# The choice of keys in a sparse-attention block: ties ranked by a running sum instead of position rounds

## The chip, the cores and the metric

The kernel runs on one core of a Trainium2 chip. A core has a matrix engine (TensorE, PE in the profile), three engines for elementwise work (VectorE or DVE, ScalarE or ACT, GpSimd or POOL) and a queue for memory transfers (SyncE, SP). Each engine takes its own instructions in order; semaphores let one engine wait for another. The metric is the device time of one execution in microseconds.

## What is computed

The block takes 1024 tokens of width 1024 through a norm and one input projection; its columns go to two mixers. One is a sparse attention: for each query a small indexer scores all keys, and the 256 keys of the highest score are kept, within the limit of the query's chunk. The other is a gated linear attention (GLA) with a recurrence over chunks. The output projection and a gated feed-forward network follow. The part that the change touches is this (of the reference):

```python
dots = jax.nn.relu(jnp.einsum('bqhd,bsd->bqhs', qib, k_idx_f) * IDX_DIM ** -0.5)
score = jnp.einsum('bqhs,bqh->bqs', dots, wb * IDX_HEADS ** -0.5)
score = jnp.where(key_pos[None, None, :] < limit, score, NEG)
_, sel = lax.top_k(score, topk)          # topk = 256
valid = sel < limit
```

Of equal scores, `top_k` keeps those of the lower position. Equal scores are frequent, because a ReLU makes many scores exactly zero.

## The kernel before

**Tiles.** The 1024 queries stand in 8 tiles of 128 partitions. `acc[t]` holds the scores of tile `t`, one row per query; its width `NA[t]` is the number of admissible keys: nothing to choose for tiles 0 and 1, then 384, 512, 640, 768, 1024 and 1024 columns for tiles 2 to 7.

**The choice.** `choose(ts)` (L739) finds for three tiles together, bit by bit, the 256th highest score of each row. It runs twice: group A is tiles 2, 5, 6 (384, 768 and 1024 columns), group B tiles 3, 4, 7 (512, 640, 1024). One round, `counts` (L758), counts for the current threshold how many scores are not below it: DVE counts the first two tiles (L756, a compare whose accumulator sums the hits), ACT the third, as a sum of signs (L762). Two compares (L776, `bit`, one for DVE's tiles and one for ACT's) turn counts into bits, and L788 builds the next threshold `thr`. There are 32 such rounds per group. Since a sum of signs counts an equal score half, `up` (L790) tries the next higher float for ACT's tile (`nxt`, one count on DVE, `keep` L807, and a predicated copy L808).

**Equal scores, before.** L817 and L819 rewrite `acc` in pieces of up to 512 columns: where the score equals the threshold the column's position from the constant `iota` (in units of 1/4096) takes its place. Then ten more rounds of the same `counts` on positions find how many are to be kept: `dlt` (L829, two compares) and `pos` (L834). L839 writes the mask into `acc[t]`, which the softmax later adds (L1340).

**The order of the work.** The program is recorded by a planner inside the kernel. Each part is a generator that yields an engine and a cost in ns, or a slot or an event to wait for; the planner runs a clock per engine and takes, among the parts that could start first, the one of the lowest rank. The order that comes out is fixed: each engine runs it as written. The planner's costs are estimates, and an edit that changes them shifts unrelated instructions. `choose` has rank 14 (`R_CHOOSE`), the projections 30, the GLA parts 2.5 to 4. Slots hold memory: `hp` hands out seven half tiles (128 partitions by 2 KB) that the choice shares with the GLA's elementwise parts.

**Names around the choice.** While the choice runs, PE computes projections (`pj`, `pf`; L368 to L370 are the three matmuls of one split product), the scores' products (`dots`), the gate of the GLA (`pz` L984), its cumulated decays (`bc` L1037), and its chunks (`pa` L1122, `pk` L1105, `pv` L1144). DVE empties what PE leaves: `la` (L987) reads `pz`, `spillq` (L876) reads `pf`, and `att` (L1124) masks `pa`. The results lie in a few banks: the next `pz` waits until `la` has read the one before, and `pk` waits until `att` has read `pa`. From `lg` (L1327) on come the softmax and the rest. At the start, `more_loads` (L427) issues small constants on SP's queue, `iota` (L435) among them, ahead of the input weights `st` (L247), which ACT (L257) and POOL (L262) split into two halves `w` for PE; `qi` is the first product with them.

Of the kernel before, what the change touches and what calls it, by code (L numbers as in the profile page):

```python
# [9 lines left out]
F32 = mybir.dt.float32  # L10
# [37 lines left out]
def f32(ap):  # L48
    return ap.bitcast(F32)
# [9 lines left out]
def dve(n):  # L59
    return n / 0.96 + 68  # L60
# [261 lines left out]
def block_kernel(ctx: ExitStack, tc: tile.TileContext, a: dict, out: bass.AP, dbg=None):  # L322
# [35 lines left out]
    def row_bc(ap, n):  # L358
        return bass.AP(tensor=ap.tensor, offset=ap.offset, ap=[[0, P], [1, n]])
# [66 lines left out]

    def more_loads():  # L427

        todo = [(mats[:, 1:, :], a["c_mats"][:, 1:, :]), (iot, row_bc(a["c_iota"], S)), (wgu[96:112, :], w_gu),
                   (bgt, row_bc(a["b_gate"], 256)), (gnb, row_bc(a["gla_norm"], 512)), (tab, a["rel_bias"]),  # L430
                   (nrm[:, 1, :], a["norm_ffn"].rearrange("l (k p) -> p (l k)", p=P))]
# [27 lines left out]


    wiT = cst.tile([P, NT * 8], F32, name="wiT")
    iot = cst.tile([P, S], F16, name="iota")
    fl = Flow()
    ev = fl.event
    pg = Slots(fl, NPG - NT - 1)
# [268 lines left out]
        yield ev("score", ORDER[-1])  # L734
        pg.give()

    UNIT = 1.0 / 4096.0

    def choose(ts):  # L739

        v = nc.vector
        n = len(ts)
        nv = n - 1
        nm = str(ts[0])
        cnt, pos, dlt = (cst.tile([P, n], F32, name=x_ + nm) for x_ in ("cnt", "pos", "dlt"))
        sgn, bit, thr = (cst.tile([P, n], I32, name=x_ + nm) for x_ in ("sgn", "bit", "thr"))
        lo, hi, cy, nxt, keep = (cst.tile([P, 1], I32, name=x_ + nm) for x_ in ("lo", "hi", "cy", "nxt", "keep"))
        thf = f32(thr)  # L750
        for t in ts:
            yield ev("score", t)

        def count(i, col, op):
            w = NA[ts[i]]
            v.tensor_scalar(junk_v[:, :w], acc[ts[i]], col, 0.0, op0=op, op1=ALU.add, accum_out=cnt[:, i:i + 1])  # L756

        def counts(col, op, after):  # L758

            t = ts[nv]  # L760
            e = yield ACT, act(NA[t], True), False
            nc.scalar.activation(junk_a[:, :NA[t]], acc[t], AF.Sign, bias=col[:, nv:], scale=-1.0,  # L762
                                 accum_out=cnt[:, nv:])
# [9 lines left out]
        def few(out_, val):  # L773

            def after(o, of_signs):
                v.tensor_scalar(out_[:, o], cnt[:, o], float(S - 2 * TOPK if of_signs else TOPK), val,  # L776
                                op0=ALU.is_gt if of_signs else ALU.is_lt, op1=ALU.mult)
            return after

        yield DVE, 70  # L780
        v.memset(thr, 0)
        yield from counts(thf, ALU.is_ge, few(sgn, -1.0))
        yield DVE, 70
        v.tensor_scalar(thr, sgn, 1 << 30, None, op0=ALU.bitwise_xor)
        for b in range(30, -1, -1):
            yield from counts(thf, ALU.is_ge, few(bit, float(1 << b)))
# [18 lines left out]
        count(nv, f32(nxt), ALU.is_ge)  # L805
        yield DVE, 200
        v.tensor_scalar(keep, cnt[:, nv:], float(TOPK), None, op0=ALU.is_ge)  # L807
        v.copy_predicated(thr[:, nv:], keep, nxt)  # L808
        for i, t in enumerate(ts):
            w = NA[t]  # L810
            for c0 in range(0, w, HB):
                o = slice(c0, min(w, c0 + HB))
                m = o.stop - o.start
                yield hp
                yield DVE, 2 * dve(m)
                tmp = half([P, HB], F32, "tie")
# [4 lines left out]
                hp.give()  # L821
        yield DVE, 140
        v.memset(pos[:, :nv], (1 + 512) * UNIT)
        v.memset(pos[:, nv:], (1 + 512 - 0.5) * UNIT)
        for b in range(9, -1, -1):
            step_ = float(1 << b) * UNIT

            def after(o, of_signs):
                v.tensor_scalar(dlt[:, o], cnt[:, o], float(2 * TOPK - S if of_signs else TOPK), step_,  # L829
                                op0=ALU.is_lt, op1=ALU.mult)  # L830

            yield from counts(pos, ALU.is_lt, after)
            yield DVE, 70
            v.scalar_tensor_tensor(pos, pos, -(step_ / 2 if b else step_), dlt, op0=ALU.add, op1=ALU.add)  # L834
        yield DVE, 70
        v.tensor_scalar(pos[:, nv:], pos[:, nv:], 0.5 * UNIT, None, op0=ALU.add)
        for i, t in enumerate(ts):
            yield DVE, NA[t] / 1.92 + 130
            v.tensor_scalar(acc[t], acc[t], pos[:, i:i + 1], BIG, op0=ALU.is_gt, op1=ALU.mult)  # L839
            save(f"mask{t}", acc[t])  # L840
            ev("mask", t).set()


    d_vb = [dr.tile([P, 512], F32, name=f"d_vb{i}") for i in range(NT)]
# [1407 lines left out]
def _constants():  # L2252
# [16 lines left out]
        "c_iota": ((np.arange(S, dtype=np.float32) + 1) / np.float32(4096.0)).astype(np.float16)[None, :],  # L2269
    }  # L2270


# [14 lines left out]
```

## Time and profile before

| | us |
|---|---|
| median of 3 runs (lowest, highest) | 1335.14 (1332.27, 1335.7) |
| profiled execution | 1333.15 |
| its span in the trace | 1331.3 |
| PE busy | 1268.2 (95% of the span) |
| DVE busy | 968.9 (73%) |
| ACT busy | 621.1 (47%) |
| POOL busy | 444.1 (33%) |

The profile shows one execution. Busy time counts an engine's instructions, not its waits, so an engine can be busy 95% on average and idle half of one stage. A wait is put down to the instruction that released it. The choice of keys runs from 94 to 409 us.

### The profile page before, as it was taken

How to read it: one execution, taken by the hardware profiler on the slowest of the kernel's cores; microseconds unless marked ns; L12 is line 12 of the kernel's file. 1: busy time of each engine (PE TensorE's matmuls, PEld its weight loads, DVE VectorE, ACT ScalarE, POOL GpSimd, SP SyncE). 2: the span in 40 equal slices, each digit the busy share in tenths (PEclk: the TensorE clock that was granted, in tenths of full speed). 3: DMA queues.
4: the chain of work that ended last, by engine and by line, in shares of the span. 5: the costliest groups of instructions: out<-in, count | busy, mean ns of one | idle time of the engine just before them, and what ended most of it. 6: DMA issues, size and time to landing. Idle time of an engine off the chain costs nothing.

```text
span 1331.3 us, 18081 instructions
## 1 busy us (share of the span) xinstructions
PE 1268.2 (95%) x6074; PEld 1028.8 (77%) x6074; DVE 968.9 (73%) x1900; ACT 621.1 (47%) x1139; POOL 444.1 (33%) x410
## 2 busy tenths in 40 slices
PE   5999999969999999989987999999999999999997
PEld 5878868746787888868865888888888888888886
DVE  5379998989996788724387788889776664435885
ACT  4467678554544677632143444444444432222232
POOL 4324324533311444561244343435333220000351
PEclk8999989979998999989988999999999999999999
DMA  7654221234471233565212676777667549555664
GB/s 217 182 145 127 67 60 49 95 127 167 170 233 46 74 112 112 164 209 206 87 40 80 221 263 235 269 263 266 221 222 237 182 170 381 200 197 190 206 252 174
DMA packets 122812, 230.22 MB, mean 173 GB/s; under 512 B 14120, under 2 KB 70240, under 8 KB 122720
## 3 DMA queue, kind: packets, MB, share of 16 engines
q1 hardware_dynamic: 122720, 229.07, 51.3%
q8 instruction: 48, 0.79, 0.3%
q14 instruction: 44, 0.36, 0.1%
HBM read 146.19 MB, written 82.85 MB: 172 GB/s over the span
## 4 chain that ended last, share of the span: by engine, by line
PE 75%; DVE 16%; issue 3%; DMA 2%; ACT 2%; POOL 1%; SPq 1%; POOLq 0%; DVEq 0%; ACTq 0%
DVE junk_v L756 6%; PE av L1387 3%; PE fc L1769 3%; PE fa L1769 3%; PE fa L1770 3%; PE fc L1770 3%; PE fa L1771 3%; PE fc L1771 3%; PE fb L1771 3%; PE fb L1770 3%; PE da L2085 3%; PE da L2083 3%; PE da L2084 3%; PE fb L1769 3%; PE ptr L1363 3%
## 5 line engine op out<-in xcount | busy, mean ns | idle before, releaser
L1594 POOL TENSOR_TENSOR w<-raw,w 128x512 fp32r<-128x512 f32 x66 | 96.8, 1469 | 181.9 <-ACT w L1730 140.7
L262 POOL TENSOR_TENSOR w<-st,w 128x512 fp32r<-128x512 f32 x68 | 91.3, 1350 | 88.3 <-ACT w L257 87.2
L1730 ACT ACTIVATE w<-raw 128x512 fp32r<-128x512 f32 x132 | 81.7, 626 | 63.0 <-DMA d_wd<-wd 17.1
L756 DVE TENSOR_SCALAR_CACHE_REDUCE junk_v<-acc,thr 128x640 bf16<-128x640 f32 (+3 forms) x128 | 103.6, 809 | 1.9
L762 ACT ACTIVATE junk_a<-acc,thr 128x1024 bf16<-128x1024 f32 x64 | 73.4, 1147 | 44.0 <-DVE thr L788 31.1
L2031 DVE TENSOR_TENSOR da<-U,da 128x512 fp32r<-128x512 f32 x54 | 43.9, 812 | 53.3 <-ACT da L2029 52.9
L1350 POOL TENSOR_SCALAR pb<-pb,sume 128x384 f32<-128x384 f32 (+3 forms) x64 | 47.6, 750 | 99.7 <-DVE sume L1348 79.9
L368 PE MATMUL pj<-w,hT 128*128 128x512 f32 x192 | 78.8, 410 | 1.4 <-DVE spillq L876 1.4
L2029 ACT ACTIVATE da<-U 128x512 fp32r<-128x512 f32 x54 | 33.6, 629 | 95.9 <-PE da L2085 28.2
L1769 PE MATMUL fb<-hc,w 128*128 128x512 f32 x176 | 70.4, 400 | 8.2 <-ACT w L1730 4.2
L368 PE MATMUL pf<-hT,w 128*128 128x512 f32 x192 | 76.7, 400 | 0.0
L1771 PE MATMUL fb<-hc,w 128*128 128x512 f32 x176 | 70.3, 400 | 5.7 <-DVE w L1597 5.7
L369 PE MATMUL pj<-w,hT 128*128 128x512 f32 x192 | 75.7, 394 | 0.0
L370 PE MATMUL pj<-w,hT 128*128 128x512 f32 x192 | 75.6, 394 | 0.0
L370 PE MATMUL pf<-hT,w 128*128 128x512 f32 x192 | 75.5, 393 | 0.0
L369 PE MATMUL pf<-hT,w 128*128 128x512 f32 x192 | 75.5, 393 | 0.0
L1770 PE MATMUL fb<-hc,w 128*128 128x512 f32 x176 | 70.7, 402 | 1.9 <-DVE hc L1597 1.2
L1594 POOL TENSOR_TENSOR wd<-wd 128x512 fp32r<-128x512 f32 x33 | 50.2, 1525 | 65.6 <-ACT wd L1960 60.1
L1960 ACT ACTIVATE wd<-wd 128x512 fp32r<-128x512 f32 x77 | 48.1, 628 | 49.9 <-DMA d_wd<-wd 22.3
L1769 PE MATMUL fc<-hc,w 128*128 128x512 f32 x176 | 68.7, 390 | 0.3 <-DVE gt L1818 0.3
L1769 PE MATMUL fa<-hc,w 128*128 128x512 f32 x176 | 68.7, 390 | 0.0
L2085 PE MATMUL da<-db,da 128*128 128x512 f32 x176 | 68.6, 390 | 0.0
(303 smaller groups left out, 3733.5 us busy)
## 6 DMA issues: line engine op xcount, KB each, us to landing
d_wd<-wd SPq DMA_DIRECT2D x77, 512.0 KB, 3.5
db<-d_wd SPq DMA_DIRECT2D x77, 512.0 KB, 3.4
st<-w_in SPq DMA_DIRECT2D x52, 256.0 KB, 2.8
raw<-w_ffn_gate SPq DMA_DIRECT2D x22, 512.0 KB, 5.2
raw<-w_ffn_up SPq DMA_DIRECT2D x22, 512.0 KB, 4.5
wd<-w_ffn_down SPq DMA_DIRECT2D x44, 256.0 KB, 4.9
d_ux<-gt SPq DMA_DIRECT2D x9, 512.0 KB, 2.6
d_uy<-gt SPq DMA_DIRECT2D x9, 512.0 KB, 2.8
```

The source lines that it names most:

```text
L262: self.nc.gpsimd.tensor_tensor(w[:, 1, :], st, f32(w[:, 0, :]), op=ALU.subtract)
L368: mm(ps, lh, rh, start=first, stop=False)
L369: mm(ps, lh, rl, start=False, stop=False)
L370: mm(ps, ll, rh, start=False, stop=last)
L756: v.tensor_scalar(junk_v[:, :w], acc[ts[i]], col, 0.0, op0=op, op1=ALU.add, accum_out=cnt[:, i:i + 1])
L762: nc.scalar.activation(junk_a[:, :NA[t]], acc[t], AF.Sign, bias=col[:, nv:], scale=-1.0, accum_out=cnt[:, nv:])
L1594: nc.gpsimd.tensor_tensor(dst, src, high, op=ALU.subtract)
L1730: nc.scalar.activation(w4[:, 0], src, AF.Copy)
L1769: mm(b, w[:, 0, kk], h[:, 0, :], start=first, stop=False, skip_group_check=True)
L1770: mm(b, w[:, 0, kk], h[:, 1, :], start=False, stop=False, skip_group_check=True)
L1771: mm(b, w[:, 1, kk], h[:, 0, :], start=False, stop=k == 3, skip_group_check=True)
L2085: mm(bs[t], l[:, 1, tt], r[:, 0, :], start=False, stop=last, skip_group_check=True)
```

## The change

The rounds lose one of their two compares: DVE's count now adds up in the unit of the sum of signs, so that a single compare of three columns serves all three tiles. It stands behind DVE's counts and behind ACT's. The tie passes and the ten position rounds go, with the constant `iota` and its load. In their place each tile gets a part of its own, `mask`, spawned with ranks 14, 15 and 16: ACT writes the sign of threshold minus score to a half tile (bfloat16) and sums it; DVE writes where the sign is zero to a second half tile (float16), makes a running sum of it in place, works out from both sums how many equal scores are too many, adds one to the sign where the running sum exceeds that number, and writes the mask.

```diff
 def more_loads():
-    todo = [(mats[:, 1:, :], ...), (iot, row_bc(a["c_iota"], S)), (wgu[96:112, :], w_gu),
+    todo = [(mats[:, 1:, :], ...), (wgu[96:112, :], w_gu),
...
 def choose(ts):
...
-        def count(i, col, op):
+        def count(i, col):
             w = NA[ts[i]]
-            v.tensor_scalar(junk_v[:, :w], acc[ts[i]], col, 0.0, op0=op, op1=ALU.add, accum_out=cnt[:, i:i + 1])
+            v.tensor_scalar(junk_v[:, :w], acc[ts[i]], col, float(S - TOPK), op0=ALU.is_ge, op1=ALU.subtract,
+                            accum_out=cnt[:, i:i + 1])
...
             for i in range(nv):
                 yield DVE, dve(NA[ts[i]]) + 70, False
-                count(i, col[:, i:i + 1], op)
-            yield DVE, 190
-            after(slice(0, nv), False)
+                count(i, thf[:, i:i + 1])
             yield At(e)
-            yield DVE, 70
-            after(slice(nv, n), True)
+            yield DVE, 150
+            v.tensor_scalar(out_, cnt, float(2 * TOPK), val, op0=ALU.is_gt, op1=ALU.mult)
...
         for i, t in enumerate(ts):
-            for c0 in range(0, w, HB):
...
-                v.scalar_tensor_tensor(tmp[:, :m], acc[t][:, o], thf[:, i:i + 1], iot[:, o],
-                                       op0=ALU.is_le, op1=ALU.mult)
-                v.scalar_tensor_tensor(acc[t][:, o], acc[t][:, o], thf[:, i:i + 1], tmp[:, :m],
-                                       op0=ALU.is_lt, op1=ALU.add)
...
-        for b in range(9, -1, -1):
...
-            yield from counts(pos, ALU.is_lt, after)
-            v.scalar_tensor_tensor(pos, pos, -(step_ / 2 if b else step_), dlt, op0=ALU.add, op1=ALU.add)
...
-            v.tensor_scalar(acc[t], acc[t], pos[:, i:i + 1], BIG, op0=ALU.is_gt, op1=ALU.mult)
+            fl.spawn(mask(t, thf[:, i:i + 1], cnt[:, i:i + 1], need[:, i:i + 1], eqs[:, i:i + 1]), R_CHOOSE + i)
...
+    def mask(t, thr, sg, need, eqs):
+        v = nc.vector
+        n = NA[t]
+        yield hp
+        yield ACT, act(n, True)
+        s = half([P, S], BF16, "sign")[:, :n]
+        nc.scalar.activation(s, acc[t], AF.Sign, bias=thr, scale=-1.0, accum_out=sg)
+        yield hp
+        yield DVE, n / 3.84 + 70
+        e = half([P, S], F16, "equal")[:, :n]
+        v.tensor_scalar(e, s, 0.0, None, op0=ALU.is_equal)
+        yield DVE, 2 * dve(n)
+        v.tensor_tensor_scan(e, e, e, 0.0, ALU.add, ALU.max)
+        yield DVE, 220
+        v.tensor_tensor(eqs, e[:, n - 1:n], sg, op=ALU.add)
+        v.tensor_scalar(need, eqs, 0.5, TOPK - n / 2.0, op0=ALU.mult, op1=ALU.add)
+        yield DVE, dve(n)
+        v.scalar_tensor_tensor(s, e, need, s, op0=ALU.is_gt, op1=ALU.add)
+        hp.give()
+        yield DVE, n / 1.92 + 70
+        v.tensor_scalar(acc[t], s, 1.0, BIG, op0=ALU.is_ge, op1=ALU.mult)
+        hp.give()
...
```

The planner moves much of the program around it. The first place is on DVE, about 250 us into the run, where group A's first tile is finished among the rounds of group B (`cnt_679`, `thr_684` and `bit_683` are group B's before; `cnt_677`, `thr_682` and `bit_681` after; `e` and `bl` belong to the GLA's decays). Before:

```order
L808 COPY_PREDICATED thr_673<-keep_678,nxt_677 128x1
L788 SCALAR_TENSOR_TENSOR thr_684<-bit_683,thr_684 128x3
L817 SCALAR_TENSOR_TENSOR tie<-acc,thr_673,iota 128x384
L819 SCALAR_TENSOR_TENSOR acc<-acc,thr_673,tie 128x384
L756 TENSOR_SCALAR junk_v,cnt_679<-acc,thr_684 128x512
L817 SCALAR_TENSOR_TENSOR tie<-acc,thr_673,iota 128x512
L819 SCALAR_TENSOR_TENSOR acc<-acc,thr_673,tie 128x512
L876 SCALAR_TENSOR_TENSOR spillq<-pf,spillq 128x512 x2
L817 SCALAR_TENSOR_TENSOR tie<-acc,thr_673,iota 128x256
L819 SCALAR_TENSOR_TENSOR acc<-acc,thr_673,tie 128x256
L756 TENSOR_SCALAR junk_v,cnt_679<-acc,thr_684 128x640
```

After:

```order
L799 COPY_PREDICATED thr_671<-keep_676,nxt_675 128x1
L755 TENSOR_SCALAR junk_v,cnt_677<-acc,thr_682 128x640
L1041 TENSOR_TENSOR e_2210<-bl,bc 128x512
L769 TENSOR_SCALAR bit_681<-cnt_677 128x3
L814 TENSOR_SCALAR equal<-sign 128x384
L779 SCALAR_TENSOR_TENSOR thr_682<-bit_681,thr_682 128x3
L816 SCALAR_TENSOR_TENSOR equal<-equal 128x384
L818 TENSOR_TENSOR eqs_668<-equal,cnt_666 128x1
L819 TENSOR_SCALAR need_667<-eqs_668 128x1
L821 SCALAR_TENSOR_TENSOR sign<-equal,need_667,sign 128x384
```

The two `spillq` evacuations stood between the tie passes and stand elsewhere now; the two small steps of a mask, `eqs` and `need`, follow its running sum (L816 in the changed kernel).

The second place is on DVE just ahead of `att` (L1124 before, L1110 after). Before, group A's position rounds (`cnt_668`, `dlt`, `pos`) alternate there with group B's:

```order
L756 TENSOR_SCALAR junk_v,cnt_668<-acc,pos_669 128x384
L756 TENSOR_SCALAR junk_v,cnt_668<-acc,pos_669 128x768
L829 TENSOR_SCALAR dlt_670<-cnt_668 128x2
L776 TENSOR_SCALAR bit_683<-cnt_679 128x1
L829 TENSOR_SCALAR dlt_670<-cnt_668 128x1
L788 SCALAR_TENSOR_TENSOR thr_684<-bit_683,thr_684 128x3
L834 SCALAR_TENSOR_TENSOR pos_669<-pos_669,dlt_670 128x3
L756 TENSOR_SCALAR junk_v,cnt_679<-acc,thr_684 128x512
L1124 COPY_PREDICATED att<-mats,pa 128x512 x2
```

After, only rounds of group B are left there:

```order
L755 TENSOR_SCALAR junk_v,cnt_677<-acc,thr_682 128x512
L755 TENSOR_SCALAR junk_v,cnt_677<-acc,thr_682 128x640
L769 TENSOR_SCALAR bit_681<-cnt_677 128x3
L1110 COPY_PREDICATED att<-mats,pa 128x512
L779 SCALAR_TENSOR_TENSOR thr_682<-bit_681,thr_682 128x3
L1110 COPY_PREDICATED att<-mats,pa 128x512
```

Up to that place DVE has, before and after: counts of 384 and of 768 columns on the threshold 32 and 32, of 512 columns 20 and 25, of 640 columns 19 and 25; compares 102 and 57; threshold steps 49 and 54; position counts of both sizes four each and none; tie pairs five and none; whole masks none and three. Up to the first `la`, 19 and 22 counts of 384 columns, 18 and 21 of 768, and 50 and 28 compares. On PE the same matmuls stand in another order: ahead of the first `pk` there are 465 rows of `pj` before and 480 after, and ahead of the fourth pair of `pz` 66 and 69 of `pf`. From the first `lg` on, the order is the same on every engine.

## Rows read from the trace of the kernel before

**Rows 1.** Waits of PE: waiting line, releaser: total us, times, longest

```profile
PE pk L1105 <- DVE att L1124: 12.5, 1, 12.5
...
PE pz L984 <- DVE la L987: 2.3, 1, 2.3
...
PE pj L368 <- DVE spillq L876: 1.4, 1, 1.4
...
PE qi L368 <- ACT w L257: 0.9, 1, 0.9
```

**Rows 2.** Busy us (x instructions) per stage; PEclk is the granted clock

```profile
250.00:278.00 28.00, 14.06 (x71) 10.68 (x70) 27.51 (x69) 14.32 (x26) 13.18 (x11) 0.81 0.41 141
278.00:295.00 17.00, 17.00 (x109) 11.55 (x109) 12.96 (x47) 7.54 (x15) 4.95 (x6) 0.91 0.23 81
328.00:350.00 22.00, 20.63 (x151) 14.33 (x152) 21.69 (x53) 10.37 (x20) 12.37 (x13) 1.00 0.54 186
```

**Rows 3.** The same view in slices of 2 us, after three waits

```profile
182.00:184.00 2.00, 1.85 (x4) 1.16 (x4) 1.97 (x9) 0.00 (x0) 0.00 (x0) 0.50 0.00 0
254.00:256.00 2.00, 0.76 (x4) 0.29 (x2) 2.00 (x2) 0.00 (x0) 0.99 (x1) 1.00 0.00 0
278.00:280.00 2.00, 2.00 (x6) 1.63 (x6) 1.93 (x6) 1.21 (x3) 0.00 (x0) 0.50 0.36 138
```

**Rows 4.** DVE in time: start, us, line, operation; group B's last position rounds

```profile
380.79 0.75 DVE L756 TENSOR_SCALAR_CACHE_REDUCE junk_v<-acc,pos 128x512 bf16<-128x512 f32 x1
...
381.58 0.88 DVE L756 TENSOR_SCALAR_CACHE_REDUCE junk_v<-acc,pos 128x640 bf16<-128x640 f32 x1
...
382.51 0.22 DVE L829 TENSOR_SCALAR dlt<-cnt 128x2 f32<-128x2 f32 x2
...
382.96 0.75 DVE L756 TENSOR_SCALAR_CACHE_REDUCE junk_v<-acc,pos 128x512 bf16<-128x512 f32 x1
```

**Rows 5.** DVE in time: group A's first position round

```profile
262.09 0.60 DVE L756 TENSOR_SCALAR_CACHE_REDUCE junk_v<-acc,pos 128x384 bf16<-128x384 f32 x1
...
262.74 1.01 DVE L756 TENSOR_SCALAR_CACHE_REDUCE junk_v<-acc,pos 128x768 bf16<-128x768 f32 x1
...
263.80 1.12 DVE L829 TENSOR_SCALAR dlt<-cnt 128x2 f32<-128x2 f32 x1
```

**Rows 6.** DVE in time: a tie pair in group A; busy us of all five

```profile
258.36 0.75 DVE L817 SCALAR_TENSOR_TENSOR tie<-acc,thr,iota 128x512 f32<-128x512 f32 x1
259.15 0.75 DVE L819 SCALAR_TENSOR_TENSOR acc<-acc,thr,tie 128x512 f32<-128x512 f32 x1
259.81 0.16 DVE L776 TENSOR_SCALAR bit<-cnt 128x2 int32<-128x2 f32 x1
...
249.70:261.45 11.75, 9.03 (x10) 1.00 0.42 133
```

**Rows 7.** DVE in time: a mask write

```profile
324.62 0.74 DVE L839 TENSOR_SCALAR acc<-acc,pos 128x1024 f32<-128x1024 f32 x1
```

**Rows 8.** All engines in time, a compare beside POOL; then busy us of L776

```profile
170.07 1.29 POOL L262 TENSOR_TENSOR w<-st,w 128x512 fp32r<-128x512 f32 x1 [5.39 <-ACT w L257]
...
170.32 1.25 DVE L776 TENSOR_SCALAR bit<-cnt 128x2 int32<-128x2 f32 x4
...
94.00:277.04 183.04, 24.04 (x102) 0.95 0.29 88
```

**Rows 9.** PE, then DVE, in time: PE's last two matmuls ahead of `pk`, and `att`

```profile
264.68 0.39 PE L369 MATMUL pj<-w,hT 128*128 128x512 f32 x1
264.91 0.40 PE L370 MATMUL pj<-w,hT 128*128 128x512 f32 x1
...
277.04 1.34 DVE L1124 COPY_PREDICATED att<-mats,pa 128x512 f32<-128x512 int32 x2
```

**Rows 10.** All engines in time at the start: a DMA issue, a weight conversion

```profile
12.94 0.46 SPq L435 DMA_DIRECT2D iota<-c_iota  x1
...
25.27 2.03 ACT L257 ACTIVATE w<-st 128x512 fp32r<-128x512 f32 x3 [4.11 <-DMA st<-w_in]
```

More of the change, by code (lines that the diff above doesn't have):

```diff
@@ L427, in more_loads @@
     def more_loads():
-        todo = [(mats[:, 1:, :], a["c_mats"][:, 1:, :]), (iot, row_bc(a["c_iota"], S)), (wgu[96:112, :], w_gu),
+        todo = [(mats[:, 1:, :], a["c_mats"][:, 1:, :]), (wgu[96:112, :], w_gu),
                    (bgt, row_bc(a["b_gate"], 256)), (gnb, row_bc(a["gla_norm"], 512)), (tab, a["rel_bias"]),
@@ L461, in block_kernel @@
     wiT = cst.tile([P, NT * 8], F32, name="wiT")
-    iot = cst.tile([P, S], F16, name="iota")
     fl = Flow()
@@ L735, in scores @@
         pg.give()
-    UNIT = 1.0 / 4096.0
     def choose(ts):
@@ L746, in choose @@
         nm = str(ts[0])
-        cnt, pos, dlt = (cst.tile([P, n], F32, name=x_ + nm) for x_ in ("cnt", "pos", "dlt"))
+        cnt, need, eqs = (cst.tile([P, n], F32, name=x_ + nm) for x_ in ("cnt", "need", "eqs"))
         sgn, bit, thr = (cst.tile([P, n], I32, name=x_ + nm) for x_ in ("sgn", "bit", "thr"))
@@ L752, in choose, with counts @@
             yield ev("score", t)
-        def count(i, col, op):
+        def count(i, col):
             w = NA[ts[i]]
-            v.tensor_scalar(junk_v[:, :w], acc[ts[i]], col, 0.0, op0=op, op1=ALU.add, accum_out=cnt[:, i:i + 1])
-        def counts(col, op, after):
+            v.tensor_scalar(junk_v[:, :w], acc[ts[i]], col, float(S - TOPK), op0=ALU.is_ge, op1=ALU.subtract,
+                            accum_out=cnt[:, i:i + 1])
+        def counts(out_, val):
             t = ts[nv]
             e = yield ACT, act(NA[t], True), False
-            nc.scalar.activation(junk_a[:, :NA[t]], acc[t], AF.Sign, bias=col[:, nv:], scale=-1.0,
+            nc.scalar.activation(junk_a[:, :NA[t]], acc[t], AF.Sign, bias=thf[:, nv:], scale=-1.0,
                                  accum_out=cnt[:, nv:])
@@ L765, in counts @@
                 yield DVE, dve(NA[ts[i]]) + 70, False
-                count(i, col[:, i:i + 1], op)
-            yield DVE, 190
-            after(slice(0, nv), False)
+                count(i, thf[:, i:i + 1])
             yield At(e)
-            yield DVE, 70
-            after(slice(nv, n), True)
[L773 to L778, printed above, removed]
+            yield DVE, 150
+            v.tensor_scalar(out_, cnt, float(2 * TOPK), val, op0=ALU.is_gt, op1=ALU.mult)
         yield DVE, 70
         v.memset(thr, 0)
-        yield from counts(thf, ALU.is_ge, few(sgn, -1.0))
+        yield from counts(sgn, -1.0)
         yield DVE, 70
@@ L785, in choose @@
         for b in range(30, -1, -1):
-            yield from counts(thf, ALU.is_ge, few(bit, float(1 << b)))
+            yield from counts(bit, float(1 << b))
             yield DVE, 70
@@ L804, in choose @@
         yield DVE, dve(S) + 70
-        count(nv, f32(nxt), ALU.is_ge)
+        count(nv, f32(nxt))
         yield DVE, 200
-        v.tensor_scalar(keep, cnt[:, nv:], float(TOPK), None, op0=ALU.is_ge)
+        v.tensor_scalar(keep, cnt[:, nv:], float(2 * TOPK), None, op0=ALU.is_le)
         v.copy_predicated(thr[:, nv:], keep, nxt)
         for i, t in enumerate(ts):
-            w = NA[t]
-            for c0 in range(0, w, HB):
[L812 to L816, printed above, removed]
-                v.scalar_tensor_tensor(tmp[:, :m], acc[t][:, o], thf[:, i:i + 1], iot[:, o],
-                                       op0=ALU.is_le, op1=ALU.mult)
-                v.scalar_tensor_tensor(acc[t][:, o], acc[t][:, o], thf[:, i:i + 1], tmp[:, :m],
-                                       op0=ALU.is_lt, op1=ALU.add)
-                hp.give()
@@ L822, in choose @@
-        yield DVE, 140
-        v.memset(pos[:, :nv], (1 + 512) * UNIT)
-        v.memset(pos[:, nv:], (1 + 512 - 0.5) * UNIT)
-        for b in range(9, -1, -1):
[L826 to L830, printed above, removed]
-            yield from counts(pos, ALU.is_lt, after)
-            yield DVE, 70
-            v.scalar_tensor_tensor(pos, pos, -(step_ / 2 if b else step_), dlt, op0=ALU.add, op1=ALU.add)
@@ L835, in choose @@
[L835 to L838, printed above, removed]
-            v.tensor_scalar(acc[t], acc[t], pos[:, i:i + 1], BIG, op0=ALU.is_gt, op1=ALU.mult)
-            save(f"mask{t}", acc[t])
-            ev("mask", t).set()
+            fl.spawn(mask(t, thf[:, i:i + 1], cnt[:, i:i + 1], need[:, i:i + 1], eqs[:, i:i + 1]), R_CHOOSE + i)
[21 more added lines that the diff above has]
+        hp.give()
+        save(f"mask{t}", acc[t])
+        ev("mask", t).set()
```

1 line of the change is left out of this document (removed).

## Prediction

> **What bounds the kernel now.** I read the waits of TensorE (PE) first, because PE has work in nearly every stage and the change touches no PE instruction: only a wait of PE can shrink. Between about 94 and 409 us, the stretch in which the choice of keys runs, three waits stand out [rows 1]: 12.5 us before `pk` (L1105), released by the VectorE (DVE) write of `att` (L1124); 2.3 us before `pz` (L984), released by `la` (L987); 1.4 us before `pj`, released by `spillq` (L876). All three end with a DVE instruction. The stage windows say why DVE is late [rows 2]: from 250 to 278 us DVE is busy 27.51 of 28 us and PE 14.06. From 278 to 295 PE never stops, and from 328 to 350 it misses 22.00 − 20.63 = 1.4 us. So the choice is worth something where it delays `att`, and almost nothing elsewhere: the rounds that follow 278 us already lie under a full PE.
>
> A wait has a second price [rows 3]. [...] The mean is 0.91 over the 17 us from 278 to 295 [rows 2], which is 17 × 0.09 = 1.5 us lost. The 1.4 us wait inside 254 to 256 left the clock at 1.00 [rows 3]. A wait at `att` that is cut but still several microseconds long therefore keeps the price; one cut below 2 us probably loses it.
>
> **What the change removes on DVE ahead of `att`.** Each position round of group B takes 382.96 − 380.79 = 2.17 us [rows 4]: a step of 0.79 for the 512 columns, 0.93 for the 640, then 0.45 of small operations (two compares of 0.12 and `pos`, 0.20). Group A's two counts step by 0.65 and 1.06 [rows 5]. Before `att`, four of group A's ten position rounds had run: 4 × 1.71 = 6.8 us of counts, and 1.8 us of `dlt` and `pos` (eight steps of 0.12, four of 0.20). The tie passes of group A cover 384 + 768 + 1024 = 2176 columns; a pair for 512 columns steps by 0.79 + 0.66 = 1.45 [rows 6], so 2176/512 × 1.45 = 6.2 us if nothing stops them; they took 9.03 us of busy time [rows 6]. Compares: 102 stand ahead of `att` before, 57 in the changed order; undisturbed, one steps by 0.12 like the `dlt` of the same form, so 45 × 0.12 = 5.4 us. Removed: 6.8 + 1.8 + 6.2 + 5.4 = 20.2 us.
>
> **What it adds there.** The planner fills the place with group B's rounds: five more counts of 512 and six more of 640, 5 × 0.79 + 6 × 0.93 = 9.5 us, and five `thr` steps of 0.20 (the form of `pos`), 1.0 us. The three masks, 2176 columns in all: `equal` 0.8 us (no row has this form on two bytes; it lies between three small steps of 0.12, 0.4, and the mask write's rate, 1.6); six small ones, `eqs` and `need`, 0.9; the add of the comparison, a pass with two inputs like L819, 2176/512 × 0.66 = 2.8; the mask write 1.4, by L839's 0.74 for 1024 columns [rows 7], less its fixed cost. The running sum is not in the trace. Its low bound is a plain two-input pass, 0.66 per 512 columns [rows 6], 2.8 us; its high bound is the slowest engine's pass over 512 columns, 1.29 [rows 8], 5.5 us. I take the low one, since that row is of the same engine and has the same operand count. Added: 9.5 + 1.0 + 0.8 + 0.9 + 2.8 + 1.4 + 2.8 = 19.2 us. DVE reaches `att` d = 20.2 − 19.2 = 1.0 us earlier. This difference of two large sums is the weak term.
>
> [...] No run here shows a scan yet.
>
> **Bounds of d.** DVE is stopped by GpSimd (POOL) in some forms and not in others: a compare that starts at 170.32, beside a POOL pass of 1.29 us from 170.07, shows 1.25 us, and the 102 compares up to 277 show 24.04 us, 0.236 each, twice the undisturbed 0.12 [rows 8]. If every compare that is gone takes its share of stops with it, 45 × 0.116 = 5.2 us more are saved; but a stop mostly ends when POOL's pass ends, whichever DVE instruction meets it, and the three merged instructions of a round stood close together, so I take none of it. The other way, the slow scan takes 2.7, and a mask's Sign on ScalarE (ACT) that comes late some 1.3. So d lies between −3 and +6, and 1.0 is taken.
>
> [...]
>
> **What moves on PE.** The changed order puts 15 `pj` matmuls more ahead of the first `pk`, that is, ahead of the wait. Two such matmuls start 0.23 us apart [rows 9], so 3.4 us of work that used to follow the wait now stand inside it. This is worth 3.4 us whenever the wait stays longer than that. The same instructions are all still there, and from the first `lg` on no engine's order differs.
>
> **The earlier waits** are no terms of their own. Ahead of `la` stand three more rounds of group A, 3 × (0.65 + 1.06 + 0.20) = 5.7 us, and 22 compares fewer, −2.6: DVE is 3.1 later, PE has three `pf` matmuls, 0.7 us, more ahead, and the wait of 2.3 becomes about 4.7. The evacuation `spillq` no longer stands behind tie passes and its 1.4 us should go. Both lie ahead of a PE that waits for `att` anyway: a microsecond lost there shortens the wait at `pk` by the same, and d already holds all DVE work up to `att`. PE would come to `pk` at 265.3 (its last matmul's end [rows 9]) + 2.4 − 1.4 + 3.4 = 269.7, and `att`, before in two instructions from 277.04 on [rows 9], would come 1.0 earlier: the wait shrinks from 12.5 to 7 or 8 us, and the clock's price stays.
>
> **After `att`** DVE has about 8 us of choice less to do up to 350, because the remaining six position rounds of group A and its three mask writes are gone; of the 1.4 us that PE misses there I take 0.5. From 350 to 409 PE is full, and the ten rounds of group B that go there (about 22 us of DVE) are worth nothing: their cover is the `pj` and `pf` work that PE has then, and PE's next wait, `lg` for the softmax, comes from DVE work that the change leaves alone.
>
> **At the start** the load of `iota` goes (0.46 us on SP's queue at 12.94, ahead of the first weight loads [rows 10]). PE waits 0.9 us at `qi` for ACT's conversion of those weights [rows 1], and ACT itself waits 4.11 us for their load [rows 10]. I take this wait in full, 0.9 us, bounded by 0 and by twice that, since POOL's share of the weights comes later with it.
>
> **The sum:** 3.4 + 1.0 + 0.5 + 0.9 = 5.8 us. The profiled execution took 1333.15 us and would take 1327.3; it lies 2.0 us under the median of the runs, 1335.14, and the same 5.8 us off the median give the forecast, **1329.3 us**. About 0.3%, 4 us, is what a measurement of this kernel can tell from no change.
>
> **The rivals.** *Forecast (chance 0.47):* d between −1.5 and +3.5, 1327 to 1332. *No gain at the wait (0.27):* d near −3, by the slow scan and stops by POOL; the sum is 3.4 − 3 + 0.5 + 0.9 = 1.8, or 1333.3, and in this case the change does on DVE nothing of what it says. For it speaks that the planner refills what is freed with other rounds. *The wait nearly goes (0.18):* d about 6 by fewer stops; the wait falls from 7 to under 2.3, the 1.5 us of half clock go as well, and 3.4 + 6 + 0.5 + 0.9 + 1.5 = 12.3 gives 1322.8. For it speak the compares' 0.236 [rows 8], against it that POOL's own work stays. *Slower (0.08):* the mask's `equal` waits on DVE for ACT's Sign, which waits for a half tile that a POOL pass still reads. Behind it on DVE are queued group B's next compare, `spillq` and the decays of the recurrence, all on the way to `att`. At two POOL passes (2 × 1.29 [rows 8]) and a Sign of about 1.0 that is 3.6 us a mask, 10.8 for the three; d becomes 1.0 − 10.8 = −9.8, and the sum is 3.4 − 9.8 + 1.4 = −5.0, or 1340.1. It decides from d = −4.8 on (no gain) and is measurable from −8.8. Against it: ACT is busy 14.32 of 28 us there [rows 2], and the masks are spread over some 20 us.
>
> **How the numbers follow.** Faster than 0.3% means under 1331.1: nearly all of the forecast's case (0.41 of 0.47) and the third, 0.59. Slower means over 1339.1: the last, 0.08. The rest, 0.33, is within. The range goes from the third case, 1321.5, up past the second with its unknown of some 3 us, 1336.5; the last case and a little at the low end stay out.
>
> **What would show it.** [...] I am wrong if `att` comes more than 3 us later or 5 us earlier than before, or if the work moved ahead of `pk` turns up as a wait further on.

## Result and the profile after

The changed kernel takes 1345.47 us (median of 5 runs, 1345.06 to 1349.63) against 1335.14 before (now five runs, 1332.27 to 1340.71): a ratio of 1.0075, interval 1.0047 to 1.0102. It is slower by some 10 us, where 5.8 us less was forecast. The profiled execution took 1345.47 us; its span is 1343.7, where that of the kernel before was 1331.3.

Waits of TensorE in the changed kernel (line, releaser: total us, times, longest), against [rows 1]; `pk` is now L1091, `pz` L970:

```profile
PE pk L1091 <- DVE thr L779: 11.0, 1, 11.0
...
PE pz L970 <- DVE la L973: 5.1, 1, 5.1
...
PE pt L1199 <- DVE keep L798: 2.0, 1, 2.0
PE pt L1199 <- DVE state L1140: 1.9, 1, 1.9
...
PE pa L1108 <- DVE ob L1175: 1.4, 1, 1.4
```

The wait before `pk` has shrunk from 12.5 to 11.0 us, that before `pz` has more than doubled, that for `spillq` is gone, and in the recurrence stand three waits that were not there or shorter. (The releaser named for `pk` is the threshold step that stands between the two halves of `att`.) The stretches around them (length, busy us of PE, its loads, DVE, ACT, POOL, then PEclk), against [rows 2, 3]:

```profile
184.50:199.00 14.50, 14.50 (x33) 10.14 (x34) 13.16 (x34) 9.70 (x16) 2.90 (x3) 0.52 0.14 36
272.00:283.00 11.00, 0.01 (x1) 0.00 (x0) 10.18 (x27) 4.96 (x8) 3.62 (x4) 0.73 0.52 185
...
310.00:324.00 14.00, 10.59 (x81) 7.26 (x79) 12.92 (x32) 3.21 (x7) 8.56 (x9) 1.00 0.59 195
324.00:352.00 28.00, 26.11 (x146) 18.21 (x145) 23.69 (x41) 9.86 (x20) 16.22 (x13) 0.82 0.48 163
```

Two things are to be seen. After the wait for `la` the clock is 0.52 over 14.5 us (before, 0.51 over the 7 us from 182 to 189): 7.0 us of work lost to the half clock and not 3.3. And from 310 to 352 PE stands idle for 5.3 us, and from 324 on its 26.1 busy us run at a mean clock of 0.82, which costs another 5 us, in a stretch where the kernel before had lost 1.6 in all. Adding what PE stood idle to what the half clock took of its busy time (busy × (1 − clock), summed over slices of 2 us), from 24 us to the first `lg`: 26.3 us before, 38.1 after. Of the 11.8 us more, 6.4 stand at `la`, 8.8 in the recurrence; `spillq` gives 1.4 back, `att` 1.0, the start 1.7; the rest is a new 0.8 us wait at 114 us. The first `lg` starts at 417.02 before and at 427.45 after: of the 12.4 us by which the two spans differ, 10.4 are there by then.

DVE in time, a whole round of group B shortly ahead of `att` in the changed kernel (start, us, line, operation):

```profile
278.13 0.75 DVE L755 TENSOR_SCALAR_CACHE_REDUCE junk_v<-acc,thr 128x512 bf16<-128x512 f32 x1
278.80 0.08 DVE L755 DVE_READ_ACCUMULATOR junk_v<-acc,thr 128x1 f32 x1
278.92 0.88 DVE L755 TENSOR_SCALAR_CACHE_REDUCE junk_v<-acc,thr 128x640 bf16<-128x640 f32 x1
279.73 0.08 DVE L755 DVE_READ_ACCUMULATOR junk_v<-acc,thr 128x1 f32 x1
279.92 0.17 DVE L769 TENSOR_SCALAR bit<-cnt 128x3 int32<-128x3 f32 x1
280.12 0.16 DVE L779 SCALAR_TENSOR_TENSOR thr<-bit,thr 128x3 int32<-128x3 int32 x1
280.31 0.75 DVE L755 TENSOR_SCALAR_CACHE_REDUCE junk_v<-acc,thr 128x512 bf16<-128x512 f32 x1
```

The round takes 280.31 − 278.13 = 2.18 us. The position round of the same widths, with two compares, took 2.17 [rows 4]. **An undisturbed round is no shorter with the merged compare:** the one that is left starts 0.19 us after the read of the last accumulator (`DVE_READ_ACCUMULATOR`) starts, and the threshold step 0.20 after it; with two compares, the same 2.17 us held both. Nor do its stops by POOL become fewer. Busy us of the compares and of the threshold steps up to `att` in the changed kernel, then the threshold steps of the kernel before:

```profile
94.00:282.23 188.23, 22.19 (x57) 0.94 0.27 84
...
94.00:282.23 188.23, 19.62 (x54) 0.94 0.27 84
```

```profile
94.00:277.04 183.04, 15.67 (x49) 0.95 0.29 88
```

57 compares cost 22.19 us where 102 had cost 24.04 [rows 8], and a threshold step went from 0.32 to 0.36 us. What POOL stops is now the next instruction in the row: in the timelines all 27 rows of compares and threshold steps that show over 0.5 us, from 94 us to `att` in the changed kernel, overlap a POOL pass. The counts are not stopped: those of 512 columns up to there take 0.73 to 0.75 us beside a POOL pass and without one.

### The profile page after: what moved, and what is told of

Same layout as the page of the kernel before. It is cut to its first block, busy times and chain, and to the rows that moved or that the text cites. A ratio compares the mean times of both kernels' runs of the same rounds, so it can differ in the third digit from the quotient of the medians.

```text
span 1343.7 us, 17903 instructions
## 1 busy us (share of the span) xinstructions
PE 1276.5 (95%) x6074; PEld 1034.2 (77%) x6074; DVE 932.6 (69%) x1700; ACT 601.8 (45%) x1111; POOL 448.7 (33%) x410
## 4 chain that ended last, share of the span: by engine, by line
PE 70%; DVE 16%; DMA 4%; ACT 4%; issue 3%; POOL 2%; SPq 1%; POOLq 0%; DVEq 0%; ACTq 0%
DVE junk_v L755 5%; PE av L1373 3%; PE da L2071 3%; PE da L2070 3%; PE da L2069 3%; PE ptr L1349 3%; PE fc L1755 3%; PE fc L1757 3%; PE fc L1756 2%; PE fa L1757 2%; PE fa L1756 2%; PE fa L1755 2%; PE fb L1757 2%; PE fb L1756 2%; PE fb L1755 2%
## 5 line engine op out<-in xcount | busy, mean ns | idle before, releaser
L755 DVE TENSOR_SCALAR_CACHE_REDUCE junk_v<-acc,thr 128x384 bf16<-128x384 f32 (+3 forms) x128 | 103.6, 809 | 2.7
L368 PE MATMUL pf<-hT,w 128*128 128x512 f32 x192 | 78.9, 411 | 0.0
L369 PE MATMUL pf<-hT,w 128*128 128x512 f32 x192 | 77.2, 402 | 0.0
L370 PE MATMUL pf<-hT,w 128*128 128x512 f32 x192 | 77.2, 402 | 0.0
```

The costliest lines, as they stand in the source:

```text
L368: mm(ps, lh, rh, start=first, stop=False)
L369: mm(ps, lh, rl, start=False, stop=False)
L370: mm(ps, ll, rh, start=False, stop=last)
L755: v.tensor_scalar(junk_v[:, :w], acc[ts[i]], col, float(S - TOPK), op0=ALU.is_ge, op1=ALU.subtract, accum_out=cnt[:, i:i + 1])
```

## The theories

The planner holds an undisturbed round of group A before for 538 + 938 + 190 + 70 + 70 = 1.81 us (two counts, two compares, a threshold step, by the costs in the code). The changed code tells it 150 for the one compare: 1.70. DVE takes 2.16 and 2.18 for these rounds where nothing stands between them (from the count of 384 columns at 134.16 us to the next at 136.32 in the kernel before, from 141.78 to 143.96 in the changed one). **Theory O:** the loss is order. A planned cost that is lower, for a round that is not, lets the planner put more rounds ahead of `la` and ahead of the recurrence's steps than DVE gets done in time. **Theory P:** the loss is the price of the new passes, the scans above all, on the way to `att` and in the recurrence.

## Experiments

All are timed beside the kernel before on the same chip; ratios are to that kernel, with 95% intervals.

| kernel | median us | ratio | interval |
|---|---|---|---|
| changed | 1345.47 | 1.0075 | 1.0047 to 1.0102 |
| x1_cost260 | 1334.32 | 0.9994 | 0.9979 to 1.0009 |
| x2_merged | 1347.9 | 1.0084 | 1.0059 to 1.0109 |
| x3_masks | 1336.78 | 0.9997 | 0.9975 to 1.002 |
| x4_noscan | 1344.26 | 1.0063 | 1.0041 to 1.0084 |
| x5_cal | 1316.42 | 0.9859 | 0.9835 to 0.9882 |
| x6_calb | 1337.83 | 1.0019 | 1.0007 to 1.0032 |
| x7_lateB | 1326.43 | 0.993 | 0.9909 to 0.995 |
| x9_both | 1321.98 | 0.9901 | 0.988 to 0.9922 |
| x10_merged260 | 1336.77 | 1.0011 | 0.9995 to 1.0027 |
| x11_before150 | 1338.67 | 1.0021 | 0.9998 to 1.0045 |
| x12_two_cal | 1311.28 | 0.982 | 0.9797 to 0.9844 |
| x13_one_cal | 1310.89 | 0.9815 | 0.9792 to 0.9838 |

### One number put back

```diff
             yield At(e)
-            yield DVE, 150
+            yield DVE, 260
             v.tensor_scalar(out_, cnt, float(2 * TOPK), val, op0=ALU.is_gt, op1=ALU.mult)
```

> The changed kernel with one number put back: the planner is told 260 ns for the merged compare (what the two compares were told together) and not 150. Not one instruction differs; on DVE 19 and 18 counts of group A stand ahead of the first la again, as in the kernel before, and not 22 and 21. Theory O (the loss is the order: the planner holds the round for cheaper than DVE runs it, and puts more rounds ahead of la): the wait of pz for la falls from 5.1 to about 2.5 us, the half clock after it from 7.0 to about 3.3 us, and since the instructions up to att hardly differ in number, att comes some 2 to 4 us earlier; 1339 us, 1336 to 1342. Theory P (the loss is the price of the new passes, which are all still there): 1344 to 1346.

1334.32 us: the whole loss is gone, without an instruction changed. That is more than theory O forecast (1336 to 1342). Its waits of TensorE:

```profile
PE pk L1091 <- DVE att L1110: 8.6, 1, 8.6
...
PE pj L368 <- ACT w L257: 4.0, 1, 4.0
...
PE pz L970 <- DVE la L973: 0.7, 1, 0.7
```

`la` comes 3.4 us earlier (180.33 and not 183.76), PE waits 0.7 us there and keeps its clock (what is lost there, half clock included, is those 0.7). Theory P can't make the loss: all new passes are in this kernel. A new wait for ACT's weights costs 4.0 us of what was won.

### Each half alone

x2_merged is the kernel before with this in its 32 threshold rounds:

```diff
-            yield DVE, 190
-            after(slice(0, nv), False)
             yield At(e)
-            yield DVE, 70
-            after(slice(nv, n), True)
+            yield DVE, 150
+            v.tensor_scalar(out_, cnt, float(2 * TOPK), val, op0=ALU.is_gt, op1=ALU.mult)
```

Its counts on DVE are those of the changed kernel. x3_masks is the changed kernel with this in `counts`:

```diff
-            yield At(e)
-            yield DVE, 150
-            v.tensor_scalar(out_, cnt, float(2 * TOPK), ...)
+            yield DVE, 190
+            v.tensor_scalar(out_[:, :nv], cnt[:, :nv], float(2 * TOPK), ...)
+            yield At(e)
+            yield DVE, 70
+            v.tensor_scalar(out_[:, nv:], cnt[:, nv:], float(2 * TOPK), ...)
```

> The kernel before with the merged compare alone (its planned cost 150); tie passes and position rounds stay. Its order has 22 and 21 counts of group A ahead of la, as the changed kernel has. Theory O: the wait for la is about 5 us with a half clock of about 7 us behind it, att comes later than in the kernel before; about 1341 us, 1338 to 1344. Theory P: none of the new passes is here, so 1334 to 1336, or a little below for 45 compares less.

> The changed kernel with two compares a round, planned as before (190 and 70): the running sum in place of the position rounds, alone. Ahead of la it has the order of the kernel before. Theory O: the wait for la is 2.3 us again; the masks cost 3 to 4 us at att by the scans, partly covered; 1335 to 1339. Theory P: all new passes are here, so nearly the whole loss is: 1342 to 1346.

The merged compare with its planned cost of 150 makes the whole loss alone (1347.9 us, above theory O's 1344), the running sum alone none that can be measured (1336.78, ratio 0.9997). Waits of TensorE in x2_merged:

```profile
PE pk L1122 <- DVE att L1141: 12.5, 1, 12.5
...
PE pz L1001 <- DVE la L1004: 5.1, 1, 5.1
```

5.1 us for `la`, as after the change, and 12.5 for `att`, as before it.

### Without the scans

```diff
-        v.tensor_tensor_scan(e, e, e, 0.0, ALU.add, ALU.max)
+        v.tensor_scalar(e[:, :16], e[:, :16], 0.0, None, op0=ALU.max)
```

> The changed kernel, order kept, with each running sum replaced by a pass over its first 16 columns: the ranking of equal scores is left out, so the time is that of the kernel without its six scans (4.9 us on DVE in group A, ahead of att, and about as much in group B). Theory P: att comes 4.4 us earlier, the waits in the recurrence shrink too, 1336 to 1341. Theory O: la still waits 5.1 us; the scans' 4.4 us are all that is won at att, 1340 to 1342, and the waits between 310 and 350 us remain, since they come from what stands ahead in the queue and not from the scans alone.

1344.26 us: at most some 1.2 us of the 10 are the scans' (ratio 1.0063 against 1.0075, intervals that overlap). `att` comes 2.6 us earlier, `la` still waits 5.2 us and `pt` 2.0, and from 308 us to the first `lg` PE is idle for 4.7 us (5.3 in the changed kernel). The waits are theory O's, the time lies 2 us above its range.

### The merged compare as such

x10_merged260 is x2_merged with the old cost, x11_before150 the kernel before with the new one (in its threshold rounds):

```diff
-            yield DVE, 150
+            yield DVE, 260
```

```diff
-            yield DVE, 190
+            yield DVE, 80
```

> The kernel before with the merged compare alone, as in x2_merged, but planned at 260 ns like the two compares that it replaces; ties and position rounds stay. Ahead of la 19 and 18 counts of group A and 9 and 9 of group B. Theory O' (a merged compare changes nothing on DVE, the loss is made by its lower planned cost alone): the 11 to 13 us that x2_merged loses are gone, 1332 to 1338. Theory C (the merged compare itself costs, since DVE has to wait for ACT and for its own accumulators before it can go on): at least half of the loss stays, 1340 to 1347.

> The kernel before, not one instruction changed, with its two compares planned at 80 and 70 ns in place of 190 and 70, 150 together as the changed kernel has. Ahead of la 19 and 19 counts of group A and 10 and 9 of group B (before 19, 18, 8, 8), ahead of att two more of each of group A, one or two more of group B. Theory O': la waits 4 to 6 us and its half clock is longer, att comes 4 to 6 us later: 1340 to 1348. Theory C: 1333 to 1337.

Planned at the old cost, the merged compare loses nothing that can be measured (1336.77, interval from 0.9995). The other way round is only half clear: the kernel before, planned at the new cost, has the long waits at the same two places (first the line of the wait for `att`, then for `la`; the compare that is named there starts 0.6 us behind `la`),

```profile
PE pk L1105 <- DVE att L1124: 11.0, 1, 11.0
...
PE pz L984 <- DVE bit L776: 5.5, 1, 5.5
```

yet its median is 3.9 us above that of the kernel before, not 5 to 13, its twelve runs lie between 1333.2 and 1348.33, and its interval holds 1. Its order is not that of the changed kernel (group B gets more rounds, group A hardly any). Where PE loses time shows the difference (idle time plus half clock, summed as above; `la` is 160 to 204 us, the recurrence 308 us to the first `lg`):

| kernel | planned for the compares, ns | at `la`, us | in the recurrence, us | up to the first `lg`, us |
|---|---|---|---|---|
| before | 190 + 70 | 5.7 | 1.7 | 26.3 |
| x3_masks | 190 + 70 | 4.0 | 1.0 | 33.3 (14.4 of them half clock behind `att`) |
| x1_cost260 | 260 | 0.7 | 4.7 | 27.3 |
| x10_merged260 | 260 | 0.8 | 1.5 | 27.8 |
| changed | 150 | 12.1 | 10.4 | 38.1 |
| x2_merged | 150 | 10.6 | 8.2 | 39.3 |
| x11_before150 | 80 + 70 | 10.7 | 1.2 | 30.6 |

The loss at `la` comes with the lower number in all three kernels that have it. The loss in the recurrence comes with it in two of them, with the running sum and without it, and not in the third. So the lower number is shown to make the longer wait for `la`; that it makes the whole 10 us in any order is not.

### Costs as DVE has them

x5_cal is the changed kernel with

```diff
-                yield DVE, dve(NA[ts[i]]) + 70, False
+                yield DVE, dve(NA[ts[i]]) + 150, False
...
-            yield DVE, 150
+            yield DVE, 400
...
             yield from counts(bit, float(1 << b))
-            yield DVE, 70
+            yield DVE, 330
```

x6_calb is the kernel before with the same counts, compares at 260 and 200 and the threshold step at 300.

> The changed kernel, the same instructions, with the planner told what a round of the choice takes on DVE in the traces (count +150 ns in place of +70, merged compare 400 in place of 150, threshold step 330 in place of 70). Ahead of la now 16 and 16 counts of group A, ahead of att 16 and 15 of group B in place of 25 and 25. Theory O (the loss is the order that too low costs make): the waits for la and att both shrink, la to under 1 us and att from 11 to 0 to 4 us, with their half clock; 1322 to 1330 us, faster than the kernel before. Rival R (the rounds that no longer stand ahead of att stand in the recurrence behind it and are paid there in the same way): the waits between 300 and 350 us grow by as much; 1333 to 1338.

> The kernel before with the same correction of the costs (count +150, compares 260 and 200, threshold step 300), ties and position rounds kept. Theory O: the kernel before, too, loses at att by too low costs; its 12.5 us wait shrinks to under 5; 1325 to 1332. If the running sum is worth anything beside the order, this stays 2 to 5 us behind the changed kernel with corrected costs. Rival R: 1333 to 1338.

x5_cal takes 1316.42 us, 29 us less than the changed kernel with the same instructions and below theory O's range. x6_calb gains nothing, where theory O forecast 1325 to 1332. The waits of TensorE, first of x5_cal, then of x6_calb:

```profile
PE pk L1091 <- DVE att L1110: 2.8, 1, 2.8
PE lg L1313 <- DVE mn L1326: 2.5, 1, 2.5
PE pt L1199 <- DVE state L1140: 1.7, 1, 1.7
```

```profile
PE lg L1327 <- DVE mn L1340: 22.3, 1, 22.3
...
PE lg L1327 <- DVE pos L824: 3.8, 1, 3.8
...
PE pk L1105 <- DVE att L1124: 0.7, 1, 0.7
```

In both, PE no longer waits for `la`, and for `att` only 2.8 and 0.7 us. But the choice now runs later, and in x6_calb it is not done when the softmax asks for the masks: PE comes to the first `lg` at 394.9, 22 us earlier than in the kernel before, but DVE's last three mask writes (L839) begin at 422.53, and `lg` waits 22.3 + 3.8 us. In x5_cal the last one (L824) is at 383.94, ahead of the first `lg`:

```profile
422.53 1.60 DVE L839 TENSOR_SCALAR acc<-acc,pos 128x512 f32<-128x512 f32 x3
```

```profile
383.94 0.69 DVE L824 TENSOR_SCALAR acc<-sign 128x1024 f32<-128x1024 bf16 x1
```

**This is what the running sum is worth in these orders:** it shortens the tail of the choice by the ten position rounds of each group, and that counts where the tail is late. The closest pair is x6_calb and x12_two_cal (below), both with two compares, planned at 460 and 400 together: 1337.83 and 1311.28 us. Rival R holds for x6_calb, though at `lg` and not in the recurrence, and falls for x5_cal.

### Group B behind `att`

```diff
         for t in ts:
             yield ev("score", t)
+        if ts[0] == 3:
+            yield ev("att", 0)
```

> The changed kernel with one wait added in the planner's program: group B's rounds begin after the first att is planned, the costs stay too low. Ahead of att stand no rounds of group B at all, and 26 and 26 counts of group A ahead of la. Theory O: la waits 3 to 6 us as in the changed kernel or longer (its rounds are still in front), att hardly waits; group B's 32 rounds, about 70 us, fall into the recurrence and the stretch up to 410, where DVE has room; 1325 to 1335. Rival R: the recurrence, whose state steps wait on DVE behind those rounds, loses what att wins; 1338 to 1346.

> Both: corrected costs, and group B begins after the first att. Theory O: la and att wait 0 to 2 us each and leave no half clock behind; 1320 to 1328. Rival R: rounds of group B in front of the state steps cost PE 8 us or more between 270 and 350; 1333 to 1340.

x7_lateB has this on the changed kernel, x9_both on x5_cal: 1326.43 and 1321.98 us. In the first `la` still waits 4.2 us, behind group A's rounds alone, and `att` 0.4. In the second none is left for `la` and 2.6 us are left ahead of `pk`, but `lg` waits 12.7 for masks: held back this far, even the shorter choice is late. Both beat the kernel before, neither beats x5_cal.

### One compare or two, nothing else moved

x12_two_cal is x5_cal with two compares planned at 260 and 140; x13_one_cal leaves the first of them out and puts the merged one at the place of the second:

```diff
             yield DVE, 260
-            v.tensor_scalar(out_[:, :nv], cnt[:, :nv], float(2 * TOPK), val, op0=ALU.is_gt, op1=ALU.mult)
             yield At(e)
             yield DVE, 140
-            v.tensor_scalar(out_[:, nv:], cnt[:, nv:], float(2 * TOPK), val, op0=ALU.is_gt, op1=ALU.mult)
+            v.tensor_scalar(out_, cnt, float(2 * TOPK), val, op0=ALU.is_gt, op1=ALU.mult)
```

> x5_cal (running sum, corrected costs) with two compares a round in place of the merged one, planned at 260 and 140, 400 together as there. It gives what the merged compare is worth once the order is not the issue. Theory O': nothing that can be told apart, 1314 to 1321. Theory C: faster than x5_cal, 1308 to 1313. If the merged compare does save its 0.12 us a round: 1320 to 1325.

> x12_two_cal with the merged compare put at the place of the second of its two compares and the first left out; the planner is still told 260 and 140, so the order is that of x12_two_cal on every engine, less one compare a round. This is the merged compare's price with nothing else moved. Theory O' (one compare less is worth nothing on DVE, since the one that is left waits for the accumulators in the same way): 1309 to 1314, not to be told from 1311.3. If a compare is worth its 0.12 us where DVE is the one waited for: 1305 to 1309. Theory C (the merged form costs, since DVE stands waiting for ACT and its own sums): 1315 to 1318.

1311.28 and 1310.89 us. The first lies in theory C's range, but the second, where only the compare differs, is theory O's: the merged compare neither costs nor gains anything that can be measured in the time. PE hardly waits for DVE in this order, so a small saving on DVE would not show there. Busy times of PE, its loads, DVE, ACT and POOL from 94 us to `att`, x12_two_cal, then x13_one_cal:

```profile
94.00:257.00 163.00, 162.36 (x733) 131.34 (x733) 146.90 (x380) 118.22 (x196) 75.41 (x57) 1.00 0.30 93
```

```profile
94.00:257.00 163.00, 162.29 (x734) 131.46 (x734) 143.35 (x332) 118.63 (x196) 75.40 (x57) 1.00 0.30 93
```

DVE is busy 3.5 us less and idle for as much more, and the time is the same. That both kernels are 5 us faster than x5_cal, at the same planned total, is order again. An order's luck is thus worth 5 us here. What speaks for the planned cost in the 10 us of the change is that all three pairs go the same way, though the third is not clear of noise: 1345.47 and 1334.32 (changed, x1_cost260), 1347.9 and 1336.77 (x2_merged, x10_merged260), 1338.67 and 1334.73 (x11_before150, the kernel before beside it). Waits of TensorE in x12_two_cal, where `la`, `att` and `spillq` make none; the first is left alone by the whole change:

```profile
PE tp L517 <- DVE x L484: 9.2, 3, 8.4
...
PE lg L1315 <- DVE mn L1328: 2.4, 1, 2.4
...
PE pt L1201 <- DVE ob L1177: 1.6, 1, 1.6
```

x13_one_cal is the version to keep: 23 us, 1.85%, under the kernel before (1334.11 beside it).

## Why the prediction was wrong

**What bounds the kernel** was read rightly for the kernel before: three waits for DVE, with a granted clock of 0.50 behind those of 2.3 and 12.5 us and of 1.00 behind that of 1.4 [rows 1, 3]; over 278 to 295 us the mean granted clock was 0.91 [rows 2]. That the choice is worth "almost nothing elsewhere" was not: most of the loss stands in the recurrence, where the trace of before showed next to none.

**The steps that failed, by size.** Against the 11.8 us that PE lost up to the first `lg`: "After `att`" forecast a gain of 0.5 us, and 8.8 were lost. "The earlier waits are no terms of their own" put them at nothing, and they cost 5.0 (6.4 at `la`, less 1.4 for `spillq`). At `att`, 3.4 + 1.0 were forecast and 1.0 came. The start gave 1.7 where 0.9 was forecast. The prediction's own sign of being wrong, `att` more than 3 us later, came true with 5.2. The first two go with the order that the lower planned cost makes: with the old cost put back (x1_cost260) PE loses 0.7 us at `la` and 4.7 in the recurrence, and not 12.1 and 10.4.

**"45 × 0.12 = 5.4 us" of compares removed** is what put d wrong. Undisturbed a merged round takes what one with two compares took (2.18 against 2.17), and the stops by POOL moved on to what was left: compares gave 1.9 us and the threshold steps took 4.0 (1.0 was forecast). Together that is 2.1 us more where 4.4 less was forecast. These 6.5 us are about the whole miss of d: `att` came at 282.23, 5.2 us later, and not 1.0 earlier, 6.2 us off. (The rest about cancels. The scans took 2.2 us more than forecast, the mask writes 1.3, and DVE stood idle 2.4 us longer ahead of the compares; the ties that are gone had taken 2.8 us more [rows 6], and `dlt` and `pos` 3.0.) The bound of −3 did not hold it, because the range let the stops of the compares only become fewer. The text had the argument in hand ("a stop mostly ends when POOL's pass ends, whichever DVE instruction meets it") and used it against a gain only.

**The running sum** was mis-sized too. The three scans of group A, in time on DVE and in a view that sums their busy time:

```profile
249.49 1.75 DVE L816 TENSOR_TENSOR_SCAN equal<-equal 128x768 f16<-128x768 f16 x1
...
261.15 2.28 DVE L816 TENSOR_TENSOR_SCAN equal<-equal 128x1024 f16<-128x1024 f16 x1
...
263.85 1.28 DVE L821 SCALAR_TENSOR_TENSOR sign<-equal,need,sign 128x1024 bf16<-128x1024 f16 x1
```

```profile
94.00:282.23 188.23, 4.99 (x3) 0.94 0.27 84
```

4.99 us and not 2.8: 2.28 us for 1024 columns, where the add of the comparison takes 1.28. That is 1.17 us per 512 columns on average (4.99 × 512 / 2176), where 0.66 was taken, and the high bound of 5.5 (the "slow scan", 5.5 − 2.8 = 2.7 more) lay nearer than the low one. But x4_noscan shows that this term weighs some 1 us in the end. The mask's own passes were stopped too; POOL, then DVE in time:

```profile
257.63 1.32 POOL L1054 TENSOR_TENSOR qk<-qk,e 128x512 f32<-128x512 f32 x1
```

```profile
257.71 1.66 DVE L824 TENSOR_SCALAR acc<-sign 128x768 f32<-128x768 bf16 x1
```

The mask write of 1024 columns, at 267.31 with POOL idle, shows 0.69 us, and this one of 768, beside a POOL pass of 1.32, shows 1.66. How the pass stops it no run here shows.

**"The earlier waits are no terms of their own"** failed as well. The wait for `la` came out as forecast (5.1, forecast 4.7), but its half clock grew with it, from 3.3 to 7.0 us, and that was left out; PE came to `pk` at 272.0 and not at 269.7. The 7.0 is one execution: in x4_noscan, with the same order, the half clock behind a wait of 5.2 us cost 3.5. In x1_cost260 the wait is 0.7 us and no half clock follows.

**"15 `pj` matmuls, 3.4 us"** did move ahead of `pk`, and the wait there shrank though `att` was 5.2 us later. But **"After `att`"**, with 0.5 us of gain forecast and 8.8 lost, took the DVE work freed in the recurrence for empty time. DVE in time, group B's end in the changed kernel:

```profile
313.64 0.16 DVE L782 TENSOR_TENSOR nxt<-thr,sgn 128x1 int32<-128x1 int32 x1
...
317.92 1.27 DVE L755 TENSOR_SCALAR_CACHE_REDUCE junk_v<-acc,nxt 128x1024 bf16<-128x1024 f32 x1
...
319.12 0.73 DVE L1110 COPY_PREDICATED att<-mats,pa 128x512 f32<-128x512 int32 x1
319.75 2.60 DVE L1193 TENSOR_SCALAR ob<-ob,rstd 128x128 f32<-128x128 f32 x4
322.27 0.71 DVE L1110 COPY_PREDICATED att<-mats,pa 128x512 f32<-128x512 int32 x1
322.88 0.13 DVE L798 TENSOR_SCALAR keep<-cnt 128x1 int32<-128x1 f32 x1
```

Before, the same count on `nxt` stood later, under a PE that was full to 409:

```profile
371.38 1.28 DVE L756 TENSOR_SCALAR_CACHE_REDUCE junk_v<-acc,nxt 128x1024 bf16<-128x1024 f32 x1
```

With the position rounds of group A gone from the recurrence, and five of group B's rounds ahead of `att`, it comes at 317.92. The second half of `att` at 322.27 stands behind the `up` chain that begins at 313.64, this count, and four steps of `ob` that take 2.60 us beside a POOL pass. There PE waits for `pa` and `pt`, 1.4 and 2.0 us, and a third wait of 1.9 follows at 347. Half clock follows the last two, about 7 and 4 us of it (the granted clock is 0.50 from 326 to 330 and from 350 to 352), so a wait "cut below 2 us" does not always lose that price. This is read from one trace: x2_merged, which keeps the position rounds, loses 8.2 us in the recurrence as well. Which instruction stands in the way there, and why x11_before150 loses no more there than the kernel before, stays open.

**The start:** PE's idle time from 24 to 32 us is 1.7 us in both profiles. The half clock that followed it before (1.7 us; mean granted clock 0.79 over these 8 us) is missing after (1.00), but x12_two_cal, without `iota` too, has it again (0.50 from 26 to 28, 0.68 from 28 to 30); whether the load was worth anything stays open.

**The rivals:** the slower one had the right sign by the wrong mechanism. `equal` never waited for its Sign in the trace. That a lower planned cost, on its own, moves the program was not among the cases, although the order showed 22 rounds ahead of `la` where 19 had stood.

## What to carry to other kernels

In a program that a planner orders, a planned cost is part of the edit: one that is lowered without the engine getting faster puts more work ahead of what others wait for. Here the gain of the shorter stage showed only once the costs were near those of the trace. Before a removed instruction is priced, look at the gap that it lay in: here a second compare, beside accumulators that had to be read anyway, added nothing to an undisturbed round (2.17 us with it, 2.18 without). And work that is freed behind a wait is refilled; ask with what.

## What the runs showed of the hardware

How long the half clock (a granted clock of 0.50) lasts after a wait differs much. In the kernel before the clock was back about 7 us after the end of a wait of 2.3 us, and under 4 us after one of 12.5; in the changed kernel 14 us after one of 5.1, and in x4_noscan, with the same order, 7 us after one of 5.2. In the profile of x3_masks, after a wait of 11.7 us, PE ran without a gap and the clock stayed at 0.50 for 27.5 us:

```profile
275.50:303.00 27.50, 27.50 (x106) 17.95 (x106) 13.90 (x45) 6.88 (x13) 6.14 (x8) 0.50 0.22 77
303.00:310.00 7.00, 7.00 (x47) 5.05 (x46) 4.15 (x15) 2.71 (x5) 0.00 (x0) 0.92 0.18 75
```

That profiled execution took 1340.04 us; the twelve runs of this kernel lie between 1329.69 (mean granted clock 0.976) and 1343.32 (0.966). What decides the length no run here shows, nor how long the half clock of the other executions was.
